# A decoder block in float32 pairs: the recurrent branch's output by seven products of halves

## The chip, the core and the metric

The kernel runs on one core of a Trainium2 chip, in one launch. The metric is the device time of that launch in microseconds; several runs of the kernel before agree within about 1 us (703.65 to 704.66, median 704.06). Every time in this text that belongs to a place in the kernel comes from one profiled execution, which took 703.83 us; the span of its instructions is 702.1 us.

The engines' short names: PE is TensorE (matmuls), PEld its weight loads, DVE is VectorE, ACT is ScalarE, POOL is GpSimd, and SP is SyncE, which only issues transfers. Each has its own queue of instructions; they wait for one another by semaphores.

## What is computed

One block for 512 tokens of width 1024: two token mixers side by side (a causal pooling mixer and a gated linear recurrence), merged by two gates, then a gated feed-forward part and a gated embedding. What matters here is the stretch from the two mixers' outputs to the start of the feed-forward part:

```python
y_pool = pool_mixer(...) @ w_pool_out               # 512x512  @ 512x1024
y_rnn = rg_lru_branch(...) @ w_rg_out               # 512x1024 @ 1024x1024
merged = gate_pool * y_pool + gate_rnn * y_rnn
x = x + rms_norm(merged @ w_o, g_mix_post)          # 1024x1024
h = rms_norm(x, g_ffn_pre)
up = h @ w_up                                       # 1024x6144
```

## The kernel before

**Arithmetic.** Operands are float32. Each is split into a rounded part and a remainder: `split` (L192) makes `hi` by a cast on ACT (L194) and `lo` by a subtraction on DVE (L190). `mm3` (L218) then makes one product from three matmuls, hi x hi, hi x lo and lo x hi (L220 to L222), with results of 128 rows and 256 or 512 columns in a PSUM bank. Weights come from DRAM as 512 KB pieces into `raw` tiles, are split in `prep` (L405, casts L435) a few pieces ahead of their use (`weight`, L445), and their slots come free when TensorE is done with them.

**Seven products of halves.** A product of two matrices that are each cut in 2 x 2 blocks takes eight block products, or seven with sums of blocks (Strassen's, in Winograd's form). The kernel before does so for `w_o` (L982 on, order `SERIAL`), for `w_up` (order `SEVEN`) and for `w_down`. The sums of weight blocks are made in DRAM by accumulating transfers on POOL's queue (`sums_of`, L276; `sum_in_dram`, L292). The sums of the other operand's blocks are made on DVE (`o_form`, L837). Results are put together in PSUM: a bank is copied by ACT into the next one's start, and DVE adds the rest. `y_rnn` is made plainly, with 8 x 8 block products of 512 columns.

**Stages.** The trace has these, in order: projections of the input, recurrence and pooling chains (to 202.64 us); the branch output, 8 tiles of output channels, each 12 matmuls for `w_pool_out` and 24 for `w_rg_out` (202.64 to 264.80), where DVE multiplies each by its gate (L879, L880) and adds the two (L881) into `mq`; the product with `w_o` (from 264.80); norms of four token tiles (`x2_norm`, `x2_out`) and their transposes (`h2_tile`, L927), between which TensorE is given small pieces of other work: `ple_tile` (L783) and the first up block, `up_plain` (L957), with the four weight pieces `PLAIN` = 11, 21, 12, 22; then the up stage, to about 545, the down stage and the end.

**The norm chain.** For a tile of tokens, ACT squares two halves with a running sum (L467), DVE adds the sums (L478), POOL raises to the power -1/2 (L462), and DVE multiplies and adds (L897, L902). The second norm repeats the squares, the sum and the power, and makes by L981 what TensorE transposes at L913. The transposed tile is split again (`C`, L194 and L190), and copied (L939). `ple_tile` empties its two banks by one copy on DVE (L793) and one on ACT (L794).

**Early splits.** Ten weight pieces are split long before their use: six of `w_o` and the four `PLAIN` ones. `split_early` (L352) loads, splits and writes both parts to DRAM (`parts`), and `prep` reads them back as two transfers. It runs in the last steps of the input stage (from step `EARLY_AT`) and once in each of the eight tiles of the branch output.

**What sets the order.** Each engine's instructions stand in a queue in the order that a planner gave them, from the order of the code, priorities (`urgent`, `high_priority`) and the links made by `behind` (L153), which puts one instruction after another on its engine. A queue goes strictly from one instruction to the next, so whatever waits holds back what stands behind it.

## Time and profile before

| what | value |
| --- | --- |
| time, median of 3 runs (lowest to highest) | 704.06 us (703.65 to 704.66) |
| time of the profiled execution | 703.83 us |
| span of its instructions | 702.1 us |
| TensorE busy | 696.5 us, 99% |
| VectorE busy | 574.1 us, 82% |
| ScalarE busy | 440.9 us, 63% |
| GpSimd busy | 82.9 us, 12% |
| branch output stage | 202.64 to 264.80, 288 matmuls of 512 columns |
| first transposes of the norm, second, third | 298.47, 307.12, 318.53 |

Rows of the time line read: start, duration, engine, line, operation, result and operands, shapes, and in brackets how long the engine stood idle before it and what released it. In groups, the number after x is a count, and the two after the bar are busy time and the mean in ns of one; the rest says what the engine waited for. The time line's starts are from the span's start. A matmul's duration is longer than the step from one to the next, since they are pipelined; the step is what counts.

### The profile page before, as it was taken

What the parts mean: (1) busy time and instruction counts of PE and PEld (TensorE: products, weight loads), DVE (VectorE), ACT (ScalarE), POOL (GpSimd) and SP (SyncE); (2) the same over time, 40 slices, a digit from 0 to 9 for tenths busy, and PEclk for the clock granted to TensorE, in tenths of its full rate; (3) what the DMA queues carried; (4) which work ended last, traced back from release to release, by engine and by line L of the source; (5) the groups of instructions that cost most, each with busy time, mean ns of one, the idle gap of its engine ahead of it and who ended that gap; (6) DMA issues with size and microseconds to landing.
All of it is one profiled execution on the core that took longest, in us unless ns stands there. A gap on an engine that the chain in (4) does not pass through costs nothing.

```text
span 702.1 us, 11239 instructions
## 1 busy us (share of the span) xinstructions
PE 696.5 (99%) x4279; PEld 637.0 (91%) x4279; DVE 574.1 (82%) x749; ACT 440.9 (63%) x670; POOL 82.9 (12%) x107
## 2 busy tenths in 40 slices
PE   9999999999999999999999999999999999999997
PEld 8888888888888888899999999999999888888886
DVE  5698645999656568777989999997999999788972
ACT  6857789953543245468866667765767766665631
POOL 0221111110000000121013232121300000001100
PEclk9999999999999999999999999999999999999999
DMA  8999986656698999996479999998976577868111
GB/s 320 406 314 244 227 229 153 157 165 219 237 327 285 323 334 374 332 317 218 152 286 240 278 297 266 304 239 299 241 200 233 203 250 235 283 206 273 47 61 60
DMA packets 65077, 172.54 MB, mean 246 GB/s; under 512 B 5952, under 2 KB 6592, under 8 KB 64704
## 3 DMA queue, kind: packets, MB, share of 16 engines
q1 hardware_dynamic: 50480, 129.88, 53.2%
q0 software_dynamic: 14400, 41.95, 25.5%
q8 instruction: 33, 0.54, 0.3%
q14 instruction: 20, 0.16, 0.1%
q10 hardware_dynamic: 144, 0.00, 0.0%
HBM read 155.03 MB, written 58.72 MB: 304 GB/s over the span
## 4 chain that ended last, share of the span: by engine, by line
PE 99%; DVE 0%; ACT 0%; issue 0%
PE ps L220 31%; PE ps L222 31%; PE ps L221 31%; PE ps L541 3%; PE ps L913 1%; PE ps L650 1%; PE ps L239 1%; PE ps L592 0%; ACT t L165 0%; DVE t L1323 0%; DVE t L1324 0%; PE ps L1034 0%; DVE m L231 0%; DVE mhalf L233 0%
## 5 line engine op out<-in xcount | busy, mean ns | idle before, releaser
L190 DVE TENSOR_TENSOR lo<-raw,hi 128x1024 fp32r<-128x1024 f32 (+2 forms) x193 | 224.0, 1184 | 60.2 <-ACT hi L435 42.3
L220 PE MATMUL ps<-A,hi 128*128 128x256 f32 (+1 forms) x608 | 194.4, 320 | 0.0
L221 PE MATMUL ps<-A,hi 128*128 128x256 f32 (+1 forms) x608 | 193.8, 319 | 0.0
L222 PE MATMUL ps<-A,lo 128*128 128x256 f32 (+1 forms) x608 | 193.8, 319 | 0.0
L435 ACT CAST hi<-raw 128x1024 fp32r<-128x1024 f32 (+1 forms) x112 | 112.0, 1011 | 80.6 <-PE ps L222 27.6
L220 PEld LDWEIGHTS ps<-A,hi 128*128 128x128 f32 x608 | 115.9, 191 | 8.2 <-issue 1.0
L222 PEld LDWEIGHTS ps<-A,lo 128*128 128x128 f32 x608 | 116.0, 191 | 6.8
L221 PEld LDWEIGHTS ps<-A,hi 128*128 128x128 f32 x608 | 116.0, 191 | 6.8
L220 PE MATMUL ps<-C,hi 128*128 128x256 f32 (+1 forms) x392 | 114.5, 292 | 0.0
L222 PE MATMUL ps<-C,lo 128*128 128x256 f32 (+1 forms) x392 | 114.3, 292 | 0.0
L221 PE MATMUL ps<-C,hi 128*128 128x256 f32 (+1 forms) x392 | 114.3, 292 | 0.0
L194 ACT CAST hi<-raw 128x1024 fp32r<-128x1024 f32 x78 | 80.3, 1050 | 24.5 <-PE ps L221 14.5
L220 PE MATMUL ps<-hi,A 128*128 128x512 f32 x224 | 85.2, 380 | 0.0
L221 PE MATMUL ps<-lo,A 128*128 128x512 f32 x224 | 84.9, 379 | 0.0
L222 PE MATMUL ps<-hi,A 128*128 128x512 f32 x224 | 84.9, 379 | 0.0
L220 PEld LDWEIGHTS ps<-C,hi 128*128 128x128 f32 x392 | 74.7, 191 | 1.9
L221 PEld LDWEIGHTS ps<-C,hi 128*128 128x128 f32 x392 | 74.7, 191 | 1.8
L222 PEld LDWEIGHTS ps<-C,lo 128*128 128x128 f32 x392 | 74.7, 191 | 1.7
L462 POOL TENSOR_TENSOR s<-s,mhalf 128x1 f32<-128x1 f32 (+1 forms) x21 | 16.2, 773 | 336.9 <-DVE s L478 315.1
L220 PEld LDWEIGHTS ps<-hi,A 128*128 128x128 f32 x224 | 42.3, 189 | 6.3 <-ACT hi L435 0.3
L222 PEld LDWEIGHTS ps<-hi,A 128*128 128x128 f32 x224 | 42.3, 189 | 6.0
L221 PEld LDWEIGHTS ps<-lo,A 128*128 128x128 f32 x224 | 42.3, 189 | 5.8
(191 smaller groups left out, 1024.0 us busy)
## 6 DMA issues: line engine op xcount, KB each, us to landing
raw<-in_w_up_dram SPq DMA_DIRECT2D x46, 512.0 KB, 7.7
wdsum<-in_w_down_dram POOLq DMA_DIRECT2D x36, 512.0 KB, 9.2
raw<-in_w_in_dram SPq DMA_DIRECT2D x32, 512.0 KB, 6.9
raw<-wdsum SPq DMA_DIRECT2D x24, 512.0 KB, 4.5
raw<-in_w_down_dram SPq DMA_DIRECT2D x18, 512.0 KB, 4.0
wosum<-in_w_o_dram POOLq DMA_DIRECT2D x12, 512.0 KB, 9.0
wdsum<-wdsum POOLq DMA_DIRECT2D x12, 512.0 KB, 6.9
parts<-hi SPq DMA_DIRECT2D x10, 512.0 KB, 5.0
```

The costliest lines, as they stand in the source:

```text
L190: return V.tensor_tensor(o, a, b, ALU.subtract)
L194: last_copy[0] = ACT.copy(hi, src)
L220: PE.matmul(o, ah, bh, start=start, stop=False, **kw)
L221: PE.matmul(o, ah, bl, start=False, stop=False, **kw)
L222: PE.matmul(o, al, bh, start=False, stop=stop, **kw)
L239: PE.matmul(wps[:, :P], ones, ones, start=True, stop=True)
L435: ins = ACT.copy(hi, raw)
L462: last_pow[0] = nc.gpsimd.tensor_tensor(y, v, mhalf[:, :n], ALU.pow).ins.name
L541: PE.matmul(rx[m], a[:, o : o + P], turns(b), start=k == 0 and i == 0, stop=k == KD - 1 and i == 2)
L650: PE.matmul(ps, bd[pr, a, o], turns(b[pr]), start=i == 0, stop=i == 2)
L913: PE.transpose(ps[:, q * P : (q + 1) * P], a[:, q * P : (q + 1) * P], ident)
```

## The change

`y_rnn` is made by the seven products too. The operand (1024 recurrent channels by 512 tokens) is cut into 2 x 2 blocks, the weight into two halves of output channels (p = 0, 1), each of 2 x 2 blocks. For each p and each product f in the order `RSEVEN`, two output tiles of 128 are made with 12 matmuls of 256 columns each (`rg_product`). ACT copies results from one bank into others, and `merge` on DVE multiplies by the gates and adds, by halves of 256 for p = 1. Around that:

- All eight `w_pool_out` products stand ahead of the first of `w_rg_out`.
- The operand's split of 8 x 512 columns goes; seven forms of 1024 columns are split, and four sums of 1024 are made on DVE. Two forms and three sums stand in the gate steps, with the sums and the fourth form's remainder placed behind the pool chain (`pool_done`); the others stand in the first five `w_pool_out` steps (`LATE_FORMS`).
- Sixteen more accumulating transfers make the sums of `w_rg_out` blocks in DRAM, at the head of POOL's queue; sums now take pieces of both p in turn. The weight has 14 pieces of 128 x 1024 instead of 8.
- The early splits are six, all of `w_o`, from step 18. The four `PLAIN` pieces of `w_up` are split where they come in the order, by the casts hi_2956, hi_3002, hi_3035, hi_3048 and the remainders lo_2957, lo_3003, lo_3036, lo_3049. No early split stands in the branch output.
- Banks of the branch output serve as the ones of `w_o`'s products; the input of the embedding is loaded after p = 0.

The core of the diff:

```diff
-EARLY_AT = 20
-SPLIT_AT = 5, 8
+EARLY_AT = 18
+FORMS_AT, RSUMS_AT = {5: 1, 12: 4}, (12, 13, 14)
...
+RSEVEN = (1, 5, 6, 2, 3, 7, 4)
...
-PLE_AT = 3
+LATE_FORMS = {0: 5, 1: 6, 2: 3, 3: 7, 4: 2}
...
     for m in range(KD):
         plan(("wpo", m), w_pool_out[m])
-        plan(("wrg", m), w_rg_out[m])
+    for p in range(2):
+        for f in RSEVEN:
+            plan(("rg", p, f), rsum[p, f] if (p, f) in rsum else rg_block(p, {1: 11, 2: 21, 3: 22}[f]))
...
-    early = [("wo", f, q) for f in SERIAL[4:] for q in range(pieces["wo"])] + [("up", 0, f) for f in PLAIN]
+    early = [("wo", f, q) for f in SERIAL[4:] for q in range(pieces["wo"])]
...
-    sum_in_dram(chain_of(sums_of("wo"), sums_of("up")), None)
+    sum_in_dram(chain_of(sums_of("rg"), sums_of("wo"), sums_of("up")), None)
...
+    def rg_sum(o, a, b, op=ALU.subtract):
+        behind(V.tensor_tensor(rg_half(*o), rg_half(*a), rg_half(*b), op), pool_done[0])
...
+    def rg_form(f):
+        if f == 3:
+            rg_sum((0, 0), (0, 0), (1, 0), ALU.add)
+        v = rg_half(*{1: (0, 0), 2: (1, 0), 4: (1, 1), 5: (1, 1), 6: (0, 0), 3: (0, 0), 7: (0, 1)}[f])
+        w = quad("C" if f in (1, 2, 4) else "A").rearrange("p (s a) (b c) -> p s (a b) c", s=2, b=2)
+        split(w[:, 0], w[:, 1], v)
+        rform[f] = w[:, 0], w[:, 1]
+        if f == 4:
+            behind(last_sub[0], pool_done[0])
...
     for m in range(KD):
         w = weight(("wpo", m))
-        pa = bank()
+        if m in LATE_FORMS:
+            rg_form(LATE_FORMS[m])
+        pas.append(bank())
         for k in range(4):
-            mm3(pa, pick(w, k * P, (k + 1) * P), yp[k], k == 0, k == 3)
-        w = weight(("wrg", m))
...
-        split_early(1)
-        pb = bank()
-        for k in range(KD):
-            y = yh[k // 4][:, k % 4, :], yl[k // 4][:, k % 4, :]
-            mm3(pb, pick(w, k * P, (k + 1) * P), y, k == 0, k == KD - 1)
...
+    def merge(p, n, i, hs):
+
+        m, c = 4 * p + 2 * n + i, hs.stop - hs.start
+        g, v = gate[8 + m][:, hs], (ra, rb2)[n][i][:, hs]
+        with urgent():
+            if n:
+                t = temp()[:, :c]
+                q = rq[p][:, None, i * HALF : (i + 1) * HALF].to_broadcast([P, c // HALF, HALF])
+                V.tensor_tensor(*(x.rearrange("p (h c) -> p h c", c=HALF) for x in (t, v)), q, ALU.add)
+                v = t
+            g4 = g.rearrange("p (h a b) -> p h a b", a=2, b=P)
+            V.tensor_tensor(g4, v.rearrange("p (h b a) -> p h a b", a=2, b=P), g4, ALU.mult)
+            V.tensor_tensor(mq[p][:, 2 * n + i, hs], gate[m][:, hs], g, ALU.add)
+
+    def rg_product(p, f):
+        for i in range(2):
+            w = weight(("rg", p, f))
+            o = {1: rz, 6: rz, 7: rz, 2: ra, 4: ra, 3: rb2, 5: (rd, rd)}[f][i]
+            a = HALF if f == 4 or (f, i) == (5, 1) else 0
+            products(o[:, a : a + HALF], w, i, rform[f], f in (1, 5), turns)
+            z = rz[i][:, :HALF]
+            with urgent():
+                if f == 1:
+                    ACT.copy(ra[i][:, :HALF], z)
+                elif (f, i) == (5, 1):
+                    rq[p] = temp()
+                    ACT.copy(rq[p], rd)
+                elif f == 6:
+                    ACT.activation(rb2[i][:, :HALF], z, AF.Identity, scale=-1.0)
+                elif f == 7:
+                    ACT.copy(ra[i][:, HALF:], z)
+                    ACT.activation(rb2[i][:, HALF:], z, AF.Identity, scale=-1.0)
+            if p and f in (2, 3):
+                merge(p, int(f == 3), i, slice(0, HALF))
+            elif f in (7, 4):
+                merge(p, int(f == 7), i, slice(HALF * p, S))
```

Three places show how the instructions stand. In these rows a name is tile_number of the program; a line of the kernel before has another number after: L190 is L191, L194 L195, L435 L449, L467 L483, L478 L494, L794 L827, L897 L975, L902 L980, L913 L991, L981 L1053, L994 L1067.

ScalarE's queue at the end of the branch output and the start of the product with `w_o`, before (A_1930, A_1931 are `mq`; ps_2450, ps_2451 the banks that product 2 goes on with):

```order
L194 CAST A_2389<-A_1930 128x1024
L435 CAST hi_2459<-raw_2457 128x1024
L435 CAST hi_2484<-raw_2482 128x1024
L194 CAST A_2420<-A_1931 128x1024
L994 COPY ps_2450<-ps_2448 128x512
L435 CAST hi_2497<-raw_2495 128x1024
L994 COPY ps_2451<-ps_2449 128x512
```

The same place after (C_2479 is `mq` of p = 1; ps_2131, ps_2132 the banks of products 1, 6 and 7, ps_2057 to ps_2117 those of the results):

```order
L946 COPY ps_2057<-ps_2131 128x256
L947 ACTIVATE ps_2097<-ps_2131 128x256
L195 CAST A_2594<-C_2479 128x1024
L946 COPY ps_2077<-ps_2132 128x256
L947 ACTIVATE ps_2117<-ps_2132 128x256
L449 CAST hi_2663<-raw_2661 128x1024
L449 CAST hi_2688<-raw_2686 128x1024
L1067 COPY ps_2057<-ps_2656 128x512
```

A cast of the next product's operand, which waits for a merge on DVE, now stands ahead of the second copy from which product 4 goes on.

VectorE's queue around the second transposes, before (m_2726 and m_2728 are what is transposed):

```order
L902 SCALAR_TENSOR_TENSOR m_2436<-t_2702,s_2712,m_2436 128x512
L902 SCALAR_TENSOR_TENSOR m_2438<-t_2703,s_2712,m_2438 128x512
L190 TENSOR_TENSOR C_2678<-ps_2766,C_2677 128x4x128
L478 SCALAR_TENSOR_TENSOR s_2722<-s_2718,s_2720 128x1
L981 SCALAR_TENSOR_TENSOR m_2726<-m_2436,s_2724,m_2427 128x512
L981 SCALAR_TENSOR_TENSOR m_2728<-m_2438,s_2724,m_2428 128x512
L190 TENSOR_TENSOR C_2680<-ps_2777,C_2679 128x4x128
L897 TENSOR_TENSOR t_2804<-ps_2448,m_2423 128x512
```

And after (m_2930 and m_2932 are what is transposed):

```order
L980 SCALAR_TENSOR_TENSOR m_2644<-t_2906,s_2916,m_2644 128x512
L980 SCALAR_TENSOR_TENSOR m_2646<-t_2907,s_2916,m_2646 128x512
L191 TENSOR_TENSOR C_2882<-ps_2972,C_2881 128x4x128
L191 TENSOR_TENSOR C_2884<-ps_2983,C_2883 128x4x128
L191 TENSOR_TENSOR lo_3003<-raw_3000,hi_3002 128x1024
L191 TENSOR_TENSOR lo_3036<-raw_3033,hi_3035 128x1024
L191 TENSOR_TENSOR lo_3049<-raw_3046,hi_3048 128x1024
L494 SCALAR_TENSOR_TENSOR s_2926<-s_2922,s_2924 128x1
L1053 SCALAR_TENSOR_TENSOR m_2930<-m_2644,s_2928,m_2635 128x512
L1053 SCALAR_TENSOR_TENSOR m_2932<-m_2646,s_2928,m_2636 128x512
L975 TENSOR_TENSOR t_3012<-ps_2656,m_2631 128x512
```

Three remainders of `w_up` weights and the second `C` split now stand between the first norm's last step and the sum s_2926.

ScalarE's queue at the copies of `ple_tile` in the third and fourth token tiles, before:

```order
L467 ACTIVATE rb,s_2923<-m_2446 128x512
L467 ACTIVATE rb,s_2933<-m_2847 128x512
L467 ACTIVATE rb,s_2935<-m_2848 128x512
L794 COPY m_2968<-ps_2960 128x512
L794 COPY m_2998<-ps_2990 128x512
```

And after:

```order
L483 ACTIVATE rb,s_3133<-m_2652 128x512
L483 ACTIVATE rb,s_3135<-m_2654 128x512
L483 ACTIVATE rb,s_3145<-m_3059 128x512
L483 ACTIVATE rb,s_3147<-m_3060 128x512
L827 COPY m_3180<-ps_3172 128x512
L195 CAST C_2881<-ps_3281 128x4x128
L827 COPY m_3210<-ps_3202 128x512
```

The four squares stand ahead of the first copy in both; a `C` cast now stands between the two copies.

More of the change, by code (lines that the diff above doesn't have):

```diff
@@ L837, in o_form @@
     def o_form(f):
-        h11, h12, h21, h22 = (halves(mq[k], b) for b in range(2) for k in range(2))
+        h11, h12, h21, h22 = (halves(mq[k], b) if k < len(mq) else None for b in range(2) for k in range(2))
         v = {1: h11, 2: h12, 4: h22}.get(f)
@@ L860, in o_lhs, with products @@
         return v[:, 0], v[:, 1]
-    mq = [quad("A", F32), quad("A", F32)]
+    def products(o, w, i, form, start, order=near):
+        for k in range(4):
+            lhs = tuple(v[:, i, k * P : (k + 1) * P] for v in w)
+            rhs = tuple(v[:, k, :] for v in form)
+            mm3(o, lhs, rhs, start and k == 0, k == 3, order, skip_group_check=True)
+    mq, pas = [], []
     for m in range(KD):
         w = weight(("wpo", m))
-        pa = bank()
+        if m in LATE_FORMS:
+            rg_form(LATE_FORMS[m])
+        pas.append(bank())
@@ L882, in block_kernel @@
-        if m == KD - 1:
-            o_form(2)
-        if m == PLE_AT:
+            mm3(pas[m], pick(w, k * P, (k + 1) * P), yp[k], k == 0, k == 3)
+        with urgent():
+            V.tensor_tensor(row(gate[m]), back(pas[m]), row(gate[m]), ALU.mult)
+    rz, rd, rq = [bank(), bank()], bank(), {}
+    ra, rb2 = pas[4:6], pas[6:8]
+    def merge(p, n, i, hs):
[10 more added lines that the diff above has]
+            V.tensor_tensor(mq[p][:, 2 * n + i, hs], gate[m][:, hs], g, ALU.add)
@@ L885, in block_kernel @@
+    for p in range(2):
+        for f in RSEVEN:
+            if f == 2:
+                mq.append(quad("C", F32))
+            rg_product(p, f)
+            if (p, f) == (1, 6):
+                o_form(1)
+            if (p, f) == (1, 7):
+                o_form(2)
+        if p == 0:
             pled = dram.tile([S, D], F32, name="pled")
@@ L949, in h2 @@
         return tuple(v[c][b] for v in (h2h, h2l))
-    def products(o, w, i, form, start):
-        for k in range(4):
-            lhs = tuple(v[:, i, k * P : (k + 1) * P] for v in w)
-            rhs = tuple(v[:, k, :] for v in form)
-            mm3(o, lhs, rhs, start and k == 0, k == 3, near, skip_group_check=True)
     def up_plain(f, b):
@@ L981, in x2_out @@
                 V.scalar_tensor_tensor(h2n[t, h], res[h], r, g_pre[h], ALU.mult, ALU.mult)
-    oz, o11, o12, od5 = ([bank(), bank()] for _ in range(4))
+    o11, o12 = ra, rb2
+    oz, od5 = ([bank(), bank()] for _ in range(2))
     o5 = wpool.tile([P, 2, S], F32, tag="sum", name=nm("sum"), bufs=1)
```

53 lines of the change are left out of this document (30 added, 23 removed).

## The prediction

> **What bounds the kernel now.** I read the page first, then the waits of TensorE, then stretches of the span by engine, and last the time lines of the places that the change touches.
>
> ```profile
> PE 696.5 (99%) x4279; PEld 637.0 (91%) x4279; DVE 574.1 (82%) x749; ACT 440.9 (63%) x670; POOL 82.9 (12%) x107
> ...
> PEclk9999999999999999999999999999999999999999
> DMA  8999986656698999996479999998976577868111
> ...
> PE 99%; DVE 0%; ACT 0%; issue 0%
> ```
>
> TensorE is busy for 99% of the span at full clock, and the chain that ended last is TensorE alone. The next lines are its waits, then four stretches: the branch output's products, 48 products of 256 columns, the mixer norm, and the up products (columns: wall, then busy time and instructions of each engine).
>
> ```profile
> PE ps L239 <- DVE mhalf L233: 1.1, 1, 1.1
> ```
>
> ```profile
> 223.36:264.80 41.44, 41.44 (x193) 36.29 (x192) 28.34 (x34) 14.61 (x17) 0.00 (x0) 1.00 0.91 317
> 302.00:325.00 23.00, 23.00 (x164) 21.67 (x163) 16.77 (x35) 18.89 (x55) 4.85 (x8) 1.00 0.94 325
> 360.00:540.00 180.00, 180.00 (x1615) 180.00 (x1614) 169.44 (x183) 122.56 (x196) 38.60 (x48) 1.00 0.95 266
> ```
>
> ```profile
> 313.17:318.53 5.36, 5.36 (x49) 5.35 (x48) 4.04 (x8) 3.72 (x11) 1.08 (x2) 1.00 1.02 370
> 444.00:484.00 40.00, 40.00 (x361) 40.00 (x360) 35.86 (x39) 25.36 (x41) 9.25 (x12) 1.00 0.99 279
> ```
>
> The only wait is one of 1.1 us at the start. So each product removed is worth its full length, and each new wait of TensorE costs its full length. VectorE is the engine with least room: it is 94% busy (169.44 of 180) right after the places of the change.
>
> **The products.** 192 matmuls of 512 columns go (8 outputs x 8 x 3) and 336 of 256 come (2 halves x 7 products x 2 x 4 x 3). The first stretch shows the pace of 512 columns: 192 matmuls (of both output weights, all of one form) in 41.44 us, 215.8 ns each. 48 of 256 columns take 5.36 us, or 111.7 ns each. New: 336 x 0.1117 = 37.52 us. The saving is 41.44 - 37.52 = 3.92 us, and it is nothing from 123.3 ns a matmul on (41.44/336).
>
> [...]
>
> **What VectorE and ScalarE get.** Durations by form:
>
> ```profile
> L190 DVE TENSOR_TENSOR lo<-raw,hi 128x1024 fp32r<-128x1024 f32 x181 | 216.4, 1220 | 47.8 <-ACT hi L435 34.7 <-ACT hi L194 7.4 <-DMA parts<-lo 2.9
> L220 PEld LDWEIGHTS ps<-A,hi 128*128 128x128 f32 x608 | 115.9, 191 | 8.2 <-issue 1.0 <-DVE lo L190 0.3
> L435 ACT CAST hi<-raw 128x1024 fp32r<-128x1024 f32 x103 | 106.7, 1045 | 58.2 <-PE ps L222 27.6 <-DMA parts<-hi 13.0 <-PE ps L221 8.2
> L1048 ACT COPY ps<-ps 128x256 f32<-128x256 f32 x22 | 7.9, 358 | 28.5 <-PE ps L222 28.5
> L881 DVE TENSOR_TENSOR A<-m,m 128x512 f32<-128x512 f32 x8 | 5.5, 686 | 0.1
> L1323 DVE TENSOR_TENSOR t<-t,A 128x256 f32<-128x256 f32 x2 | 0.9, 426 | 2.8 <-ACT t L165 2.8
> ```
>
> Back-to-back rows overlap by about 0.08 us, so a row costs its queue 1.14 us at 1024 columns, 0.60 at 512 and 0.345 at 256. Output: 24 merges of 512 (14.4 us) become 8 of the pool branch, 10 of 512 and 20 of 256 (4.8 + 6.0 + 6.9 = 17.7 us). Weights: 8 splits become 14, +6.8 us on VectorE and +5.7 on ScalarE (0.95 each). Operand: 8 splits of 512 become 7 of 1024 and 4 sums of 1024, 4.8 against 12.5 us; five splits and one sum of them lie after 202.64. The eight early splits that ran here go (-9.1 us). With the rest, from 202.64 to the new end of the stage VectorE gets about 14 + 3 wo splits (19.4), wpo splits 3.6, forms 6.8, merges 17.7, sundries 2.3: some 50 us in 58, 85%, where 223.36 to 264.80 shows 28.34 of 41.44, 68%. That hides, except where a copy that TensorE awaits stands behind something late. I find three such places before the norm:
> - First half, product 7 to 4: a weight cast of ScalarE waits for product 7 and stands ahead of the copy (L946): 0 to 0.3 us, taken 0.1.
> - Second half, product 4: the cast of o form 2 (A_2594) waits for VectorE's merge C_2479, done at some 258.7 behind splits and merges; 0.95 us of cast and the copy follow, so the copy ends at 260.1 against 259.6 due: 0.5.
> - Mixer product 2: the copy of bank 1 (L1067) stands behind the cast A_2719. Before, the copy left TensorE only 0.53 us:
>
> ```profile
> 270.18 0.57 ACT L994 COPY ps<-ps 128x512 f32<-128x512 f32 x1 [0.19 <-PE ps L222]
> ```
>
> ```profile
> 271.28 0.38 PE L220 MATMUL ps<-hi,A 128*128 128x512 f32 x1
> ```
>
> A cast of 0.95 us that starts some 0.7 us before the copy could leaves 0.1 to 0.5: taken 0.3. So the mixer's later products run about 3.92 - 0.1 - 0.5 - 0.3 = 3.0 us earlier than before; I use 2.8, with the wait of the chain behind the first copies.
>
> **The four up weights, split late.** Before, the PLAIN up weights were split early, written as parts and read back. Now their four casts and four lo (L191) stand in the mixer norm. Before, there:
>
> ```profile
> 298.11 0.15 DVE L478 SCALAR_TENSOR_TENSOR s<-s,s 128x1 f32<-128x1 f32 x1
> ...
> 299.34 1.41 DVE L902 SCALAR_TENSOR_TENSOR m<-t,s,m 128x512 f32<-128x512 f32 x2 [0.43 <-POOL s L462]
> 301.42 0.69 DVE L190 TENSOR_TENSOR C<-ps,C 128x512 fp32r<-128x512 f32 x1 [0.67 <-ACT C L194]
> 302.04 0.16 DVE L478 SCALAR_TENSOR_TENSOR s<-s,s 128x1 f32<-128x1 f32 x1
> 302.85 1.42 DVE L981 SCALAR_TENSOR_TENSOR m<-m,s,m 128x512 f32<-128x512 f32 x2 [0.66 <-POOL s L462]
> 304.19 0.68 DVE L190 TENSOR_TENSOR C<-ps,C 128x512 fp32r<-128x512 f32 x1
> 304.79 0.68 DVE L897 TENSOR_TENSOR t<-ps,m 128x512 f32<-128x512 f32 x1
> ```
>
> ```profile
> 307.12 1.04 PE L913 MATMUL ps<-ident,m 128*128 128x128 f32 x8
> ```
>
> L981 (L1053 after) makes the two inputs of the transposes at 307.12, ready at 304.27, and L897 (L975) empties the bank of the second four, at 305.47: 1.6 us or more to spare. After, the transposes are due at 307.12 - 2.8 = 304.3, the second four at 304.7. VectorE in the new order: the norm step s_2914 (before 298.11) would stand at 295.3, but two weight splits now stand ahead of the step before it, one sum more ahead of itself, and POOL's 0.85 us (302.04 to 302.85) is uncovered: some 296.9. lo_2957 covers the next step of POOL: 298.2. Two L980, 1.35: 299.5. Two C splits, 1.2: 300.7. Three weight splits, 3.45: 304.15. L494 and POOL, 0.85: 305.0. L1053 twice and L975, 0.66 + 0.66 + 0.62: 306.9. The wait is 306.9 - 304.7 = 2.2 us. Its bounds: 0, if the gaps of 0.43 to 0.67 and the span ahead absorb the splits, and 3.5, all three splits on the path. I take 2.2, because the queue is in order and the rows price every step.
>
> **The next copy.** The up product 12 (319.32) needs the bank that L794 (L827) empties, and ScalarE's order puts four squares ahead of that copy:
>
> ```profile
> 314.02 1.41 DVE L902 SCALAR_TENSOR_TENSOR m<-t,s,m 128x512 f32<-128x512 f32 x2 [0.66 <-POOL s L462]
> ```
>
> ```profile
> 314.86 0.63 ACT L467 ACTIVATE rb<-m 128x512 f32<-128x512 f32 x1 [1.49 <-DVE m L902]
> ...
> 317.19 0.64 ACT L467 ACTIVATE rb<-m 128x512 f32<-128x512 f32 x1
> 317.73 0.19 ACT L467 ACTIVATION_READ_ACCUMULATOR rb<-m 128x1 f32 x1
> 317.82 1.06 ACT L794 COPY m<-ps 128x512 f32<-128x512 f32 x2
> ```
>
> ```profile
> 319.32 0.36 PE L220 MATMUL ps<-C,hi 128*128 128x256 f32 x1
> ```
>
> The first of the two copies ends 4.4 us after L902 starts (318.4), 0.9 before its use. After, TensorE wants the bank at 319.32 - 2.8 + 2.2 = 318.7. VectorE goes on from 306.9: L494, POOL under two L826 copies 308.2; L980 308.9; two C 310.1; L980, L975 311.4; POOL 312.4; L1053, L975, L1053 314.3; lo_3229, now ahead of the norm step, 315.5; L494 and POOL 316.3; then 4.4 us: 320.7. Wait: 2.0 us, bounds 0 (in step with TensorE, as before) and 3.5. I take 2.0. Two shorter waits of the up stage's start (a copy behind a split, 1.0 us of slack before) get 0.3, bounds 0 to 1.5.
>
> **Transfers and POOL.** 16 sums of w_rg_out (512 KB) join the head of POOL's queue; 8 part writes and 8 reads leave SP's, and 6 weight loads join. The next thing on POOL is the norm's step:
>
> ```profile
> POOL s L462 <- DVE s L478: 160.4, 12, 132.9
> ```
>
> ```profile
> ACT hi L435 <- DMA parts<-hi: 20.8, 5, 5.9
> ```
>
> POOL idles 132.9 us before that step, so 16 sums are covered even at 8 us of queue each (128 us). The 20.8 us in which ScalarE waits for part writes go, and are worth nothing to a TensorE that did not wait. The transfers are 8 to 9 tenths busy in the first 100 us both ways; four sums at once may push a weight load: 0 to 2 us, taken 0, since the slots were as full with other sums. The sums of halves behind the pool chain leave VectorE 2 splits and 3 sums of 1024 instead of 8 splits of 512 beside it: 0.
>
> **Sum.** -3.92 + 0.1 + 0.5 + 0.3 + 0.2 (the rounding to 2.8) + 2.2 + 2.0 + 0.3 = +1.7 us. The profiled execution took 703.83 us, 0.23 under the median, so 705.5 on its frame and 705.7 as a median.
>
> **Rivals.** A change within 0.2% (1.4 us) is about what a measurement of this kernel can't tell from none.
> - Faster, by one mechanism: the late splits find VectorE ahead. If lo_3003, lo_3036 and lo_3049 finish by 301.9 rather than 304.15 (a wait of nil at the transposes), lo_3229 is early too, and only the 0.9 to 1.1 us of the copies stay: 704.06 - 3.92 + 1.2 = 701.3. For it: VectorE idles 0.43, 0.67 and 0.66 us around 300, and is 73% busy from 302 to 325. Against: the splits stand in the queue ahead of the step, not in its gaps, and two of them wait for casts that wait for TensorE to free the slots.
> - One of the two norm waits alone: -3.92 + 1.1 + 2.1 = -0.7, 703.3, no change. For it: after the first, TensorE is 2.2 us later, which gives the second chain time.
> - The backlog stays: VectorE at 85% in the output stage and 94% in the up stage cannot catch up, and four more waits of 0.5 to 1 us stand at its merges and splits, 2.8 us in all: 708.5. For it: 169.44 of 180 us busy. Against: casts and splits of weights run ahead there, with TensorE never waiting.
> - The 256-column products do not get the pace: if the weight loads can't be overlapped, each takes the 191 ns of the load's row, 64.2 us for 336, +22.7: 726. Against: 40.00 us hold 360 such products. [...]
>
> **Chances.** Forecast 0.36 (slower 0.30, same 0.06), faster rival 0.31 (0.30 faster), one wait 0.16 (0.13 same, 0.03 faster), backlog 0.16, pace 0.01. So faster 0.33, same 0.20, slower 0.47. The forecast's own range is 704.3 to 707.5. The whole: from 701.0, the faster rival with a little less copy wait, to 708.5, the backlog.
>
> **What would show it.** The products of the branch output at 111.7 ns and a stage that begins the mixer 3 to 4 us earlier confirm the first step. The waits of TensorE would list ps of L991 behind VectorE's m of L1053 or t of L975, about 2 us, and ps of L222 behind ScalarE's L827, about 2 us; waits behind L946 and L1067 below 0.6 us. If neither of the two large ones is there, the forecast is wrong and the time is near 701; if TensorE waits for transfers before 150 us, or for splits after 330 us, it is wrong the other way.

## The result, and the profile after

The changed kernel is slower: 708.51 us (median of four runs, 707.81 to 710.24) against 704.3 us (the kernel before, median of four), a ratio of 1.0064 with a 95% interval of 1.0044 to 1.0085. That is 4.2 us more, where 1.7 us was forecast, and just beyond the upper end of the range. The profiled execution took 708.84 us, its span is 707.1 us.

The page of the changed kernel, engines and chain:

```profile
PE 696.1 (98%) x4423; PEld 639.3 (90%) x4423; DVE 592.0 (84%) x772; ACT 456.0 (64%) x693; POOL 95.1 (13%) x123
...
PE 84%; DVE 8%; ACT 3%; issue 2%; DMA 1%; POOL 1%; SPq 0%; ACTq 0%; DVEq 0%
```

TensorE is busy as long as before (696.1 against 696.5 us), although its products became shorter (1.7 us of it is what a stretch at half clock adds, shown below), and the chain that was all TensorE now has 8% of VectorE. The waits of TensorE (who, the line waited for, us in total, times, longest) name the places; before there was only the one of 1.1 us behind mhalf:

```profile
PE ps L991 <- DVE m L1053: 1.6, 1, 1.6
PE ps L222 <- ACT ps L946: 1.1, 1, 1.1
PE ps L241 <- DVE mhalf L235: 1.1, 1, 1.1
PE ps L222 <- ACT ps L1119: 0.8, 1, 0.8
PE ps L991 <- DVE s L494: 0.5, 1, 0.5
PE ps L557 <- ACT A L527: 0.5, 1, 0.5
PE ps L222 <- ACT ps L1067: 0.3, 1, 0.3
PE ps L222 <- DVE sum L1350: 0.3, 1, 0.3
PE ps L557 <- ACT hi L446: 0.2, 1, 0.2
```

Three stretches by engine (wall, then busy time and instructions of PE, PEld, DVE, ACT and POOL, granted clock, share of DMA, GB/s): the new products of the branch output, the norm, and the matmuls behind the second transposes.

```profile
223.95:263.00 39.05, 37.98 (x337) 37.64 (x336) 36.62 (x50) 24.31 (x38) 0.00 (x0) 1.00 0.91 321
303.00:325.00 22.00, 19.82 (x124) 17.56 (x123) 18.30 (x31) 16.13 (x42) 2.89 (x6) 0.92 0.66 227
309.39:312.74 3.35, 3.35 (x10) 2.69 (x9) 3.35 (x7) 2.40 (x8) 0.15 (x1) 0.51 0.92 346
```

The 336 products of 256 columns fill the 37.98 us in which TensorE was busy in the first stretch: 113 ns each, against 111.7 priced. VectorE, though, is busy for 36.62 of 39.05 us, 94%, where it was 68% before. Over the whole stage (203.23 to 263.03) it is 53.33 of 59.80 us, 89%, where 85% was forecast: 80% up to 223.95, and 94% from there. The groups by form from these products to beyond the second transposes (223.36 to 322 us before, 223.95 to 325 after) show with what; before, then after:

```profile
L190 DVE TENSOR_TENSOR lo<-raw,hi 128x1024 fp32r<-128x1024 f32 x19 | 23.2, 1220 | 12.6 <-ACT hi L435 12.6
```

```profile
L191 DVE TENSOR_TENSOR lo<-raw,hi 128x1024 fp32r<-128x1024 f32 x28 | 33.5, 1217 | 2.2 <-ACT hi L449 2.2
```

Nine weight remainders of 1024 columns more, 10.3 us of VectorE's time, and the 12.6 us in which VectorE used to stand idle for want of a cast shrink to 2.2.

**Where the time went.** The matmuls of the two kernels can be paired from the mixer product on. The difference of their starts (after minus before) tells what each place cost:

| place (start before, start after) | lost or won there, us | forecast, us |
| --- | --- | --- |
| first loads of the kernel, code that did not change | +0.59 | 0 |
| products of the branch output | -3.92 | -3.92 |
| copy L946, second half | +1.24 | +0.5 |
| small steps up to the mixer product (264.80, 263.03) | +0.32 | +0.3 |
| copy L1067 (271.28, 270.00) | +0.60 | +0.3 |
| second transposes, both halves (307.12, 307.74) | +1.79 + 0.74 | +2.2 |
| eight matmuls at half pace | +1.74 | 0 |
| copy L827 (319.32, 322.64) | +0.21 | +2.0 |
| start of the up stage: L1174 (340.38, 343.93), L1119 (347.14, 351.66) | +0.34 + 0.87 | +0.3 |
| sum of L1350 and small steps, to 641.63 | +0.41 | 0 |

They add up to 4.93 us at 641.63, and the spans differ by 5.0. The first row is no part of the change: in the profiles of the experiments below it lies between -0.5 and +1.2 us, taken 65 us into the kernel.

The time lines of the places. ScalarE in front of the mixer product:

```profile
260.21 1.05 ACT L195 CAST A<-C 128x1024 fp32r<-128x1024 f32 x1 [1.70 <-DVE C L928]
261.17 0.37 ACT L946 COPY ps<-ps 128x256 f32<-128x256 f32 x1
```

The cast of o form 2 waits 1.70 us for VectorE's merge and holds the copy that TensorE needs. VectorE in the norm:

```profile
299.95 1.42 DVE L980 SCALAR_TENSOR_TENSOR m<-t,s,m 128x512 f32<-128x512 f32 x2 [0.43 <-POOL s L478]
301.28 1.43 DVE L191 TENSOR_TENSOR C<-ps,C 128x512 fp32r<-128x512 f32 x2
302.63 3.49 DVE L191 TENSOR_TENSOR lo<-raw,hi 128x1024 fp32r<-128x1024 f32 x3
306.04 0.15 DVE L494 SCALAR_TENSOR_TENSOR s<-s,s 128x1 f32<-128x1 f32 x1
306.85 1.41 DVE L1053 SCALAR_TENSOR_TENSOR m<-m,s,m 128x512 f32<-128x512 f32 x2 [0.66 <-POOL s L478]
```

The three remainders lo_3003, lo_3036 and lo_3049 stand in one piece of 3.49 us ahead of the norm step at 306.04. TensorE meanwhile:

```profile
305.73 0.38 PE L224 MATMUL ps<-hi,m 128*128 128x512 f32 x1
307.74 0.63 PE L991 MATMUL ps<-ident,m 128*128 128x128 f32 x4 [1.63 <-DVE m L1053]
308.92 0.82 PE L991 MATMUL ps<-ident,m 128*128 128x128 f32 x4 [0.55 <-DVE s L494]
309.39 0.77 PE L222 MATMUL ps<-hi,m 128*128 128x512 f32 x1
309.96 0.63 PE L223 MATMUL ps<-lo,m 128*128 128x512 f32 x1
310.38 0.63 PE L224 MATMUL ps<-hi,m 128*128 128x512 f32 x1
```

The second four transposes waited for their bank; the profile names the row behind the one that empties it (L975, which ends at 308.86). Between the end of the last product (306.11) and the next (309.39) lie 3.3 us with eight transposes only. Eight matmuls follow at half pace, most at steps of 427 ns, twice the 216 ns of before, at a granted clock of 0.51 (the stretch counts two of the transposes too).

### The profile page after: what moved, and what is told of

It reads as the page before. It is cut to its first block, busy times and chain, and to the rows that moved or that the text cites. A ratio compares the mean times of both kernels' runs of the same rounds, so it can differ in the third digit from the quotient of the medians.

```text
span 707.1 us, 11612 instructions
## 1 busy us (share of the span) xinstructions
PE 696.1 (98%) x4423; PEld 639.3 (90%) x4423; DVE 592.0 (84%) x772; ACT 456.0 (64%) x693; POOL 95.1 (13%) x123
## 4 chain that ended last, share of the span: by engine, by line
PE 84%; DVE 8%; ACT 3%; issue 2%; DMA 1%; POOL 1%; SPq 0%; ACTq 0%; DVEq 0%
PE ps L222 27%; PE ps L224 26%; PE ps L223 26%; PE ps L557 3%; DVE lo L191 2%; ACT rb L483 1%; PE ps L666 1%; DMA m<-in_x_t_dram 1%; DVE A L191 1%; POOL s L478 1%; DMA m<-in_rows_dram 1%; DVE m L1180 1%; DVE t L975 1%; DVE m L927 1%; ACT hi L195 1%
## 5 line engine op out<-in xcount | busy, mean ns | idle before, releaser
L191 DVE TENSOR_TENSOR lo<-raw,hi 128x1024 fp32r<-128x1024 f32 (+2 forms) x199 | 230.4, 1183 | 44.2 <-ACT hi L449 29.1
L222 PE MATMUL ps<-A,hi 128*128 128x256 f32 (+1 forms) x672 | 212.2, 316 | 0.8 <-ACT ps L1119 0.8
L223 PE MATMUL ps<-A,hi 128*128 128x256 f32 (+1 forms) x672 | 211.4, 315 | 0.0
L224 PE MATMUL ps<-A,lo 128*128 128x256 f32 (+1 forms) x672 | 211.4, 315 | 0.0
L449 ACT CAST hi<-raw 128x1024 fp32r<-128x1024 f32 (+1 forms) x118 | 118.3, 1013 | 57.0 <-PE ps L224 30.1
L222 PEld LDWEIGHTS ps<-A,hi 128*128 128x128 f32 x672 | 128.2, 191 | 9.3 <-issue 1.0
L224 PEld LDWEIGHTS ps<-A,lo 128*128 128x128 f32 x672 | 128.3, 191 | 6.9
L223 PEld LDWEIGHTS ps<-A,hi 128*128 128x128 f32 x672 | 128.2, 191 | 6.7
L222 PE MATMUL ps<-C,hi 128*128 128x256 f32 x376 | 103.7, 276 | 1.1 <-ACT ps L946 1.1
L224 PE MATMUL ps<-C,lo 128*128 128x256 f32 x376 | 103.2, 274 | 0.0
L223 PE MATMUL ps<-C,hi 128*128 128x256 f32 x376 | 103.2, 274 | 0.0
L195 ACT CAST hi<-raw 128x1024 fp32r<-128x1024 f32 x78 | 80.6, 1052 | 28.1 <-PE ps L223 18.3
L222 PEld LDWEIGHTS ps<-C,hi 128*128 128x128 f32 x376 | 71.8, 191 | 1.8 <-ACT ps L946 1.3
L223 PEld LDWEIGHTS ps<-C,hi 128*128 128x128 f32 x376 | 71.8, 191 | 0.1
L478 POOL TENSOR_TENSOR s<-s,mhalf 128x1 f32<-128x1 f32 (+1 forms) x21 | 15.2, 725 | 329.1 <-DVE s L494 306.4
L307 POOL DMA_DIRECT2D wdsum<-in_w_down_dram x36 | 33.3, 1087 | 110.2 <-ACT ps L1114 53.4
```

The source lines that it names most:

```text
L191: return V.tensor_tensor(o, a, b, ALU.subtract)
L195: last_copy[0] = ACT.copy(hi, src)
L222: PE.matmul(o, ah, bh, start=start, stop=False, **kw)
L223: PE.matmul(o, ah, bl, start=False, stop=False, **kw)
L224: PE.matmul(o, al, bh, start=False, stop=stop, **kw)
L307: ins = nc.gpsimd.dma_start(o, i, **kw)
```

## The experiments

**The theory** is that the four remainders of the up weights, which the change moved into the norm, cost what the products save, because each stands in VectorE's queue ahead of something that TensorE waits for. **The rivals** are: the order of casts and copies on ScalarE (L946, L1067), the half clock, and a saving of the products that never arrives.

### The late splits alone, with the plain product

In the kernel before, only the list of early splits is shortened:

```diff
-    early = [("wo", f, q) for f in SERIAL[4:] for q in range(pieces["wo"])] + [("up", 0, f) for f in PLAIN]
+    early = [("wo", f, q) for f in SERIAL[4:] for q in range(pieces["wo"])]
```

> The kernel before with the six early splits of w_o alone, the four up weights split late, w_rg_out as before. Theory A: TensorE waits in the norm or the first up products also here, 705 to 708 us. Theory B (only beside the seven products does it cost): within 1 us of before, 703.5 to 705 us.

Measured: 709.97 us, ratio 1.0081 (1.0068 to 1.0094). One part of the change, without the products, costs 5.8 us, at least as much as the whole change. TensorE's only new wait is this one, and then the clock (the stretch begins with the second matmul after it):

```profile
PE ps L220 <- ACT m L794: 3.9, 1, 3.9
```

```profile
323.92:326.50 2.58, 2.58 (x14) 2.58 (x14) 2.46 (x6) 2.00 (x5) 0.54 (x1) 0.54 0.75 275
```

The wait of 3.9 us is behind the copy that the prediction named (L794 before, L827 after): three remainders stand in one piece from 306.55 to 310.04, another (317.35) ahead of a norm step, and that step's multiply starts at 319.29 instead of 314.02; the squares and the copy come after it. The half clock adds 1.6 us by the starts. Against this kernel, the products win 1.5 us by the medians, which is not clear of the noise (709.29 to 710.64 against 707.81 to 710.24).

### The early splits put back

Four more pieces are split early again, in the last four `w_pool_out` steps:

```diff
+    early = [("wo", f, q) for f in SERIAL[4:] for q in range(pieces["wo"])] + [("up", 0, f) for f in PLAIN]
...
+        split_early(1 if m >= 4 else 0)
```

> The changed kernel with ten early splits again: the four PLAIN up weights are split in pool-branch steps 4 to 7 of the branch output, written as parts and read back. Theory A (the late up splits make the waits at the second transposes, 1.6 + 0.5 us, and these the low clock after them): no wait at the transposes, no low clock, the saving of the products stays, 699.5 to 702 us, faster than before by 2 to 4. Theory B (the seven products themselves load VectorE so that the norm is late whatever the weights do): waits of 1 us or more stay at the transposes, 705 to 708 us.

Measured: 714.18 us, ratio 1.0136 (1.0121 to 1.0151). The waits of the norm are gone, and a longer one has come:

```profile
PE ps L222 <- ACT ps L940: 5.4, 1, 5.4
```

```profile
229.03 1.05 ACT L195 CAST hi<-raw 128x1024 fp32r<-128x1024 f32 x1 [5.70 <-DMA parts<-hi]
```

A cast of an early split waits 5.70 us until the parts of an earlier one are written out, and the copy that TensorE needs stands behind it. The run settles where the splits can't go, not what they cost. Four more runs, all with ten early splits, had the same outcome. In the first, all ten go into the last six gate steps, one, one and then two a step:

```diff
-        split_early(1 if n >= EARLY_AT else 0)
+        split_early(2 if n >= 20 else 1 if n >= EARLY_AT else 0)
```

> The changed kernel with ten early splits, all of them in the last six gate steps (one, one and then two a step); none in the branch output. Theory A (the late up splits make the norm's waits): no wait at the second transposes or at L827, and none of the 5.4 us of the first such kernel if the gate steps have the room; the waits at L946 and L1067 stay: 703 to 705.5. Theory B (the seven products' own load on VectorE): TensorE waits 2 us or more in the branch output or the norm also here, 706.5 or more.

Measured: 721.19 us, ratio 1.0239 (1.0225 to 1.0253), with

```profile
PE ps L222 <- ACT hi L449: 12.9, 2, 7.0
```

that is, weights of `w_pool_out` which come late: the load issued at 207.62 stands in SP's queue behind six part writes (from 200.47 on). The second adds to it the two links on ScalarE of the next section (and the next form's cast behind its copy):

```diff
+                behind(last_copy[0], seven_done[0])
...
+                if f == 2:
+                    behind(last_copy[0], one_done[0])
```

> As the kernel with ten early splits in the gate steps, with the two casts of o forms put behind the copies from which TensorE's next product goes on (A_2594 behind product 7's, the next form's behind the mixer product 1's). If those two casts are the cause of the waits at L946 and L1067: both below 0.3 us, 1 to 2 us less than without, 701 to 703.5, faster than the kernel before. If VectorE's lateness is: the wait moves to the next product and the time stays within 0.5 us.

Measured: 719.36 us, ratio 1.0226 (1.0203 to 1.0249): L449 12.0 us, while the waits of L946 and L1067 and those of the norm are absent. In the third, the up weights go first, one per step from gate step 14:

```diff
-EARLY_AT = 18
+EARLY_AT = 14
...
-    todo = list(early)
+    todo = early[6:] + early[:6]
```

> As the kernel with both (ten early splits in gate steps, two casts behind the copies), but the four up weights first and one split a step over the last ten gate steps. If the waits of 6.5 and 6 us of that kernel came of two splits a step, whose part writes stood in SP's queue ahead of the next loads: they fall below 2 us in all, no low clock, and the rest stays as it was there (no wait in the norm): 701 to 703.5, faster than before. If the gate steps have no room for ten at any pace: 706 or more.

Measured: 718.85 us, ratio 1.0192 (1.0169 to 1.0215), with waits of 9.4 us behind L449 and 3.4 us behind remainders, where less than 2 us in all was expected. In the fourth, they are spread over `w_pool_out` steps 1, 4 and 7 and the first half's product 5:

```diff
+        split_early(1 if m in (1, 4, 7) else 0)
...
+            if (p, f) == (0, 5):
+                split_early(1)
```

> Six early splits in the gate steps as in the changed kernel; the four up weights split in pool-branch steps 1, 4 and 7 and after the first half's product 5, some 8 us apart; the two casts behind the copies. Theory: the part writes have landed before their slots are wanted, VectorE has room for one split per 8 us: waits below 1.5 us in the branch output, none in the norm, 701 to 703.5. Rival: VectorE's load in the branch output is too high for four more splits (4.6 us): waits of 3 us or more there, 704 to 707.

Measured: 715.06 us, ratio 1.0147 (1.0129 to 1.0164), with waits of 4.2 us behind L940 and 3.9 us behind L947. Four places for the early splits in five runs, none with a wait at the norm's transposes, all slower than the change. Neither the gate steps nor the branch output with the new products had room for them in any of these ways; that no place has is not shown.

### The order on ScalarE

The cast of o form 2 is put behind product 7's last copy:

```diff
+                    seven_done[0] = ACT.activation(rb2[i][:, HALF:], z, AF.Identity, scale=-1.0).ins.name
...
+                behind(last_copy[0], seven_done[0])
```

> The changed kernel with the cast A_2594 of the second o form put behind the last copies of product 7 on ScalarE. The wait of 1.2 us at L946 goes down to 0.2 or less. If TensorE alone sets what follows: 1 us less, 707.3. If VectorE's queue sets the norm, as I read the trace: the mixer's products start 1 us earlier, the wait at the second transposes is longer by as much, and the time stays within 0.4 us of the changed kernel, 708.1 to 708.9.

Measured: 708.26 us, ratio 1.0063 (1.005 to 1.0075): no gain, though the wait behind L946 is gone. Its waits (L1068, L1054 and L1120 are L1067, L1053 and L1119 of the changed kernel):

```profile
PE ps L222 <- ACT ps L1068: 1.8, 1, 1.8
PE ps L992 <- DVE m L1054: 1.6, 1, 1.6
...
PE ps L222 <- ACT m L827: 1.6, 1, 1.6
PE ps L222 <- ACT ps L1120: 0.8, 1, 0.8
```

The wait moved on to the next copy, 0.3 to 1.8 us. That copy, too, stands behind a cast that waits for VectorE:

```profile
268.36 1.04 ACT L195 CAST A<-C 128x1024 fp32r<-128x1024 f32 x1 [1.69 <-DVE C L878]
```

In the changed kernel this cast starts at 268.42: VectorE sets it, wherever TensorE is. The run has a second use: with the same wait of 1.6 us at the transposes it has no half clock,

```profile
309.39:312.74 3.35, 3.35 (x18) 2.95 (x17) 3.35 (x7) 2.44 (x8) 0.11 (x1) 1.00 0.88 327
```

and yet up product 12 starts at 322.55, against 322.64 in the changed kernel. What the clock did not take, the wait behind L827 took (1.6 us instead of 0.21): the half clock cost the changed kernel nothing. Its four runs say the same: the two at a mean granted clock of 1.000 took 710.24 and 708.18 us, those at 0.996 and 0.997 took 708.84 and 707.81.

The gap ahead of the slow matmuls, 3.4 us from 305.95, when the next product was due, to 309.39, was filled directly too. Six matmuls of 512 columns, whose result is thrown away, go ahead of the second transposes:

```diff
+                for _ in range(6):
+                    PE.matmul(ps, pq[0][0][:, :P], pq[0][0], start=True, stop=True)
```

> The changed kernel with six matmuls of 512 columns ahead of the second transposes, into the bank that the transposes then overwrite; their results are used by nothing. They fit into the wait of 1.8 us (6 x 0.216 = 1.3 us). Theory C (the ten matmuls at 427 ns after the transposes are a clock that fell because TensorE made no products for 3.4 us): those run at 216 ns, the waits stay or grow a little, 1.5 to 1.8 us less than the changed kernel, 706.5 to 707.2. Rival D (the low pace has another cause, such as late weights): the same pace of 427 ns, 708 to 710.

Measured: 706.62 us (median of five: three at 706.1 to 706.6, two at 708.1 and 708.7), ratio 1.0042 (1.003 to 1.0054). The profiled execution is the slowest, 708.71 us: before the new products it is already 2.16 us behind the kernel before, where the changed kernel is 0.59 behind. The half pace is absent in it (mean granted clock 0.998 over the execution, where the changed kernel has 0.996; 1.000 in the other four runs), but the planner also put lo_3229 behind the last norm's multiply, and a multiply of the norm ahead of two `C` remainders, so the 1.9 us can't be put down to the clock. The next run moves lo_3229 alone, without the link of the cast:

```diff
+        added[0] = ins.ins.name
...
+        if p == 1 and f == 1:
+            behind(last_sub[0], added[0])
```

> The changed kernel with one remainder, lo_3229 (a weight of the first up block by seven products), put behind the last norm's multiply on VectorE; the late splits of the four PLAIN weights stay. Theory A' (VectorE's queue sets the copy L827, and that copy sets where TensorE goes on at the up product 12, so low clock and waits ahead of it are given back there): 1 to 1.5 us less than the changed kernel, 706.8 to 707.5. Rival (TensorE's own loss at the transposes and the low clock set the time): within 0.4 us of the changed kernel, 708.1 to 708.9.

Measured: 708.16 us, ratio 1.0059 (1.0047 to 1.0071), with 0.5 us behind the bank's copy, where the run of the cast, also at full clock (a mean of 0.999 here, 1.000 there) but without this link, has 1.6: the remainder did stand in the way there. The whole time can't be told from the changed kernel's, as the rival said.

### All small repairs together, the late splits kept

The two links of the last section, and the next form's cast behind its copy:

```diff
+                behind(last_copy[0], seven_done[0])
...
+                if f == 2:
+                    behind(last_copy[0], one_done[0])
...
+            behind(last_sub[0], added[0])
```

> The changed kernel, late up splits kept, with all three orders mended: A_2594 and the next form's cast behind the copies on ScalarE, lo_3229 behind the last norm's multiply. If these orders were most of the loss: 704 to 705.5. If the four late splits on VectorE's queue in the norm are, as the theory has it: the waits at the second transposes grow by what is gained ahead of them, 706.5 to 708.

Measured: 706.4 us over eight runs, ratio 1.0032 (1.0022 to 1.0042), 2.1 us better than the changed kernel. Now the mixer product starts 3.92 us earlier than in the kernel before, of which 3.7 were won in the stage itself (its first loads are 0.2 us early). So the third rival falls: the saving of the products arrives. These waits spend it:

```profile
PE ps L995 <- DVE m L1057: 1.7, 1, 1.7
PE ps L222 <- issue: 1.2, 1, 1.2
...
PE ps L222 <- ACT ps L1125: 0.8, 1, 0.8
PE ps L995 <- DVE t L978: 0.5, 1, 0.5
PE ps L222 <- ACT m L829: 0.5, 1, 0.5
```

From -3.92 us the difference climbs by 1.35 at the wait for "issue" (in the mixer product, at 282.9), 2.62 at the transposes, 0.8 at up product 12 and 1.38 up to 347, to +2.23.

Next, the three remainders go behind the second norm's multiply, so that the transposes come first:

```diff
+        if p == 0 and f != 11 and normed:
+            behind(last_sub[0], normed[0])
```

> The kernel with the three orders mended, and the remainders of three late up weights (21, 12, 22) put behind the second norm's multiply on VectorE; the same work, another order. Theory A (those remainders ahead of the norm step are what TensorE waits for at the second transposes): the waits of 1.7 and 0.5 us there fall below 0.3; the third norm is then later by some of the 3.4 us of the three, so part of it comes back at the up product 12: 0.8 to 2.2 us less than the 706.4 of the kernel without this, 704.2 to 705.6. Rival (the norm is late for other reasons): the waits stay above 1 us, 706 to 707.

Measured: 707.55 us, ratio 1.0047 (1.0034 to 1.0061). Neither forecast fits: the transposes wait 0.4 instead of 2.2 us, as in theory A, but as much and more has come up further on (L831 is the bank's copy), and the time is not better:

```profile
PE ps L222 <- ACT m L831: 2.0, 1, 2.0
...
PE ps L223 <- DVE C L191: 0.8, 1, 0.8
```

One more link, product 7's sum behind the latest remainder, was meant for the wait for "issue":

```diff
-            V.tensor_tensor(v, h11, h21, ALU.subtract)
+            behind(V.tensor_tensor(v, h11, h21, ALU.subtract), last_low[0])
```

> As the one before, and the sum for the mixer's product 7 put behind the remainder of the form for product 3, which TensorE waits 1.35 us for at the mixer's product 3. Theory (VectorE's queue, 3.9 us shorter of time than before, sets that start): the wait falls below 0.5 us, and the time by 0 to 1.2 us more, 703.2 to 705.2: even with the kernel before. Rival: the wait only moves to product 7 or to the norm, the same time as the one before.

Measured: 707.63 us, ratio 1.0048 (1.0035 to 1.0061). That wait fell from 1.1 to 0.7 us, the time did not. The profile names no releaser of it, but the starts point to one. In the kernel with all small repairs:

```profile
282.16 1.29 DVE L1083 TENSOR_TENSOR ps<-sum,ps 128x512 f32<-128x512 f32 x2
282.95 0.45 PE L222 MATMUL ps<-hi,A 128*128 128x512 f32 x1 [1.18 <-issue]
```

L1083 is VectorE's subtraction into the banks that product 3 goes on with; the first of the two, some 0.69 us long, ends 0.10 us before TensorE starts. The distance is the same 0.10 us in the two runs after it, in the one with both links and early splits, and in the last one below. So it is most likely VectorE's queue again: this subtraction, which stands behind the remainder that the expectation named.

### The four remainders left out

Both kernels leave out a part of the computation: the remainders of the four late up weights aren't made, and TensorE reads the rounded parts in their place. TensorE runs as many matmuls as before, and VectorE has four subtractions less.

```diff
-        split(hi, lo, t)
+        if p == 0:
+            last_copy[0] = ACT.copy(hi, t)
+            lo = hi
+        else:
+            split(hi, lo, t)
```

> The changed kernel without the remainders of the four PLAIN up weights: the four VectorE subtractions are left out and TensorE reads the rounded part in their place, so the first up block is computed without the low parts; all else is as it was. Theory A (the remainders in VectorE's queue make the norm's waits and what follows): no wait at the second transposes or at L827, 3 to 4.5 us less than the changed kernel, 704 to 705.5. Rival (VectorE is late from the branch output on, with or without them): 1 us of wait or more stays in the norm, 706 to 708.

Measured: 703.53 us over eleven runs, ratio 0.9991 (0.9982 to 1.0). That is 5.0 us below the changed kernel, for four instructions of 1.14 us on VectorE, 4.6 us of its queue. The casts of these weights stand within 0.3 us of where they stand in the changed kernel, so it is not they that cost it. One thing moved along: with the four gone the planner puts lo_3229 behind the third norm's multiply, as in the kernel before, and the 5.0 us hold what that is worth. All waits of TensorE in this run:

```profile
PE ps L222 <- ACT ps L950: 1.1, 1, 1.1
PE ps L241 <- DVE mhalf L235: 1.1, 1, 1.1
PE ps L561 <- ACT hi L450: 0.7, 1, 0.7
PE ps L222 <- ACT ps L1123: 0.6, 1, 0.6
PE ps L222 <- ACT ps L1071: 0.3, 1, 0.3
PE ps L561 <- ACT A L531: 0.2, 1, 0.2
```

No wait is left in the norm, the granted clock is 1.00 from 303 to 325, and up product 12 starts 0.96 us before that of the kernel before, where the changed kernel is 3.31 us behind: 4.3 of the 5.0 us are won up to there. The copies L946 and L1067 (here L950 and L1071) wait as they did. With the small repairs as well:

> The same four subtractions left out of the kernel with three mended orders (706.4). Theory A: the waits in the norm go, those at the mixer's product 3 (1.35) and in the up stage (1.4) stay: 706.4 less 3.0 (1.9 + 0.7 + 0.8, less some 0.4 that moves on), 702.5 to 704.5, at or under the kernel before. Rival: 705.5 or more.

Measured: 702.76 us, ratio 0.9978 (0.9969 to 0.9987). The mixer product starts 3.75 us earlier than before; 1.3 go at the wait for "issue", 0.7 at the start of the up stage. So even with those remainders gone, the saving of 3.92 us comes out as 1.5. Against the kernel with all small repairs, in which a link holds lo_3229 at the same place, the four remainders alone are worth 3.6 us.

No version that computes everything beats the kernel before.

## Why the prediction came out as it did

The chain of causes was right in the main, its sizes were not. The step that failed is the load of VectorE in the new branch output, "some 50 us in 58, 85% … That hides, except where a copy that TensorE awaits stands behind something late". It was 89%, and 94% in the half with the merges, and the terms that hang on VectorE's lateness were sized too small: copy L946 0.5 instead of 1.24 us, the start of the up stage 0.3 instead of 1.21, and three others by 0.3 to 0.4 each.

- **The products** ("the saving is 41.44 - 37.52 = 3.92 us"): right. The pace is 113 ns in the changed kernel, and with the repairs on ScalarE 3.7 us arrive at the mixer product.
- **Copy L946** ("the copy ends at 260.1 against 259.6 due: 0.5"): the right place and mechanism, mis-sized: 1.24 us. The cast started at 260.21 instead of at 258.7, since VectorE's merge was later. An average over the stage hid that the half with the merges is at 94%.
- **Copy L1067** ("taken 0.3"): 0.6, beyond its bound of 0.5. The removal of the first wait raised it to 1.8 us. Both have two conditions: a cast that waits for VectorE, and the order on ScalarE that puts it ahead of the copy. With both casts put behind the copies both waits are gone, although VectorE has no less work.
- **The transposes** ("the wait is 306.9 - 304.7 = 2.2 us"): right in the mechanism: 2.5 us were lost, behind L1053 and the empty bank as said, with three remainders in one piece. That the size came out is in part luck, since both sides of the difference were later: the remainders were done at 306.04 instead of 304.15, and TensorE was due at 305.95 instead of 304.3.
- **The next copy** ("wait: 2.0 us"): the sum of the place is right, its make-up not. 1.95 us went, 1.74 of them as matmuls at half clock, which were not foreseen, and 0.21 as the wait. Where the clock stayed full and the order was the same, 1.9 us went there, 1.6 of them as the wait: the copy set that place, as said.
- **The start of the up stage** ("Two shorter waits of the up stage's start … get 0.3"): the term most off, 1.2 us. The copy L1119 stands behind four casts of weights on ScalarE, but so it did before (L1046); before, then after:

```profile
342.93 3.89 ACT L194 CAST hi<-raw 128x1024 fp32r<-128x1024 f32 x4
346.72 0.64 ACT L1046 ACTIVATE ps<-ps 128x256 f32<-128x256 f32 x2
```

```profile
347.43 3.91 ACT L195 CAST hi<-raw 128x1024 fp32r<-128x1024 f32 x4
351.23 0.65 ACT L1119 ACTIVATE ps<-ps 128x256 f32<-128x256 f32 x2
```

The whole run of work is 4.5 us later, where TensorE is 3.3 to 3.7 us later. It starts with a copy that waits for VectorE's t of L1129 (1.56 us; before, for the same row, 1.08), which is 4.51 us later too. The forecast went by "1.0 us of slack before". That is the slack of the first copy (done at 339.38, used at 340.38); the second one had none: its first half is done at 347.06, and TensorE was due at 347.08. Without the four remainders 0.7 us stay here, since TensorE comes 0.96 us earlier than before and this copy only 0.22.

- **After that**, 0: the sum of L1350 and small steps cost 0.41, and the first loads, which are not the change's, 0.59 in this profile.

The terms that were too small are L946 by 0.7, L1067 by 0.3, the transposes by 0.3, the up stage by 0.9 and the end by 0.4: 2.6 us, about the distance between measured and forecast (4.2 against 1.7). The rival of the backlog (2.8 us more, 708.5) is the nearest: L946, L1067 and the start of the up stage wait for work that VectorE does late. That its 708.5 is the measured time almost to the digit is luck: it had four waits of 0.5 to 1 us, and what came is one of 0.7, one of 0.9 and three smaller ones. The argument against it, that casts and splits run ahead in the up stage, did not hold at its start. The faster rival, splits that find VectorE ahead, is refuted by the remainders' run: without those remainders the time falls by 5.0 us.

## What to carry to other kernels

When TensorE is given less to do in a stage, the other engines' queues have less time for the same work there (VectorE went from 68% to 94% beside the new products): count their instructions for the shortened stretch, part by part, and not as an average over the stage. A wait that is taken away can come back at the next consumer while the engine behind it is late, as it did here at L1067 (0.3 to 1.8 us, with the wait behind L946 gone) and at the bank's copy (0.21 to 1.6 us, with the half clock gone). The three orders together brought back 2.1 us, four instructions less on the late engine 3.6 us more. Comparing the start times of the same matmuls in both traces shows this in one table, where a list of waits shows only who came last.

## What was not expected of the hardware

After the second transposes the granted clock was 0.51 for 3.35 us: eight matmuls, most at steps of 427 ns. In the 3.3 us ahead TensorE had done eight transposes and waited. With the late splits alone it was 0.54 after a wait of 3.9 us. Three other runs had the same transposes and waits of 1.6 to 1.7 and 0.5 us at the same place, without a low clock: 1.00 from 309.39 to 312.74 with the cast behind the copy (3.2 us between the products there), 1.00 from 303 to 325 with all small repairs, and a mean of 0.999 over the execution with lo_3229 alone. So of four like cases one was followed by the low clock. What sets it off is not shown by a run here; that it is the time without products was a theory, and the run with six matmuls in the gap can't settle it, since other instructions moved in it as well.

What it cost hung on what followed: 1.6 us with the plain product, and nothing in the changed kernel, where the next copy was later than the slow matmuls (up product 12 starts at 322.64 with them, at 322.55 without).
